# A mixer and feed-forward layer on one core: a conditioning row loaded later, conditioning steps loaded one ahead, and six reloads moved beside the last attention head

## The chip, the cores and the metric

The kernel runs on one core of a Trainium2 chip. The metric is the device time of one execution in microseconds (us); three runs of the kernel before gave a median of 1257.21 us (1256.59 to 1258.64).

## The reference, cut to what matters

One layer of a diffusion backbone over 512 latent tokens of width 1024, with a context of 256 tokens, all in float32. The conditioning vector `c` gives six modulation vectors; two are needed at once, the other four (first gate, second shift, second scale, second gate) only from the output projection on.

```python
mod = (silu_c @ w_ada[l] + b_ada[l])[:, None, :]
sh1, sc1, g1, sh2, sc2, g2 = jnp.split(mod, 6, axis=-1)
...
hm = head_norm(h_f + h_b, lp["m_norm_g"]) * o      # two-way mLSTM, four heads
hh = hyena(hv, (hx1, hx2), spec, lp["hy_skip"])    # long convolution, two orders
y = gm * (hm @ lp["w_pm"]) + gh * (hh @ lp["w_ph"])
return y @ lp["w_out"]
...
x = x + g1 * y
h2 = rmsnorm(x, norm2_g[l]) * (1.0 + sc2) + sh2
x = x + g2 * swiglu(h2, ffn_w1[l], ffn_w3[l], ffn_w2[l])
return rmsnorm(x, final_g)
```

## The kernel before, in words

Activations are held with features on the 128 partitions and the 512 tokens along the free axis, so a matrix of width 1024 is eight tiles of 128 x 512. Every product of two float32 matrices is made of three matmuls on operands split into a high and a low part (`mm3`, L214 to L217): ACT copies the high part, DVE subtracts it for the low part (`split`, L210 to L212). A tile of a projection (`gemm`) is 8 k-steps of three matmuls, 24 matmuls of 512 columns.

Weights come through `wsplit` (L221): a raw tile `wr` of 512 KB is loaded from SP's queue (L236), then split into `wh` and `wl`. Each of the three tags has four buffers. The `wr` buffers are also the staging slots of all other things that are split or used once: the heads' q, k and v (L886), and the conditioning steps. So at most four such loads are in flight or waiting to be used, whoever wants them.

The order on each engine is set by a scheduler in the program's build: it takes instructions by priority, which is the order in which the program makes them, with the loads and splits of weights 600 places ahead. In the trace the loads into `wr` leave SP in the program's order. Each queue then runs strictly in the order that was fixed. `issue_after` (`behind`) holds a group of instructions behind a given matmul of the same engine.

The stages that matter here, in order:

- **The Hyena convolution** in four channel blocks, in pool `ph`. Its last act is the store of two tiles `cx` into DRAM (hhd, L1237, from POOL's queue). Then the pool is closed (L1238) and its memory is given to the tile `crow` (pool `pc`) and to the heads' pool `pm`. The pool `pm` waits tile by tile for what lay there before (`reuse_waits="tile"`); `pc` waits for the whole of `ph`.
- **The conditioning row.** `ada_row` (L352) loads `c` broadcast to all partitions into `crow` (L354), takes a tanh on ACT into a `wr` slot (L355) and makes silu with two DVE instructions (L356, L357). It stands right behind the closing of the pool (L1240).
- **The conditioning steps.** `ada_later` (L339) is a generator: each `next` loads 512 KB of `w_ada` into a `wr` slot (L344), multiplies it by `crow` on DVE and adds it up along the free axis (L346, with a read of the accumulator). `background()` does one step; 24 steps are spread over the tiles of w_ph (8), w_pm (8) and w_out (5, then 3 at once), and 8 more over the first tiles of the feed-forward layer.
- **Left-over gate tiles.** Of the 28 tiles of q and gates that serve as fillers, six are left at the end of the Hyena stage; they are put between the loads, the decays and the scores of head 0 (`fill(next(cf))`, counts 2, 1, 0, 1, 1, 1). `sel` and `mask` are small tables that the decay rows need (L1280 to L1285); the decay rows are the matmuls L854.
- **The heads** (loop over `h`, L1315). `start(h + 1)` loads and splits the next head's q, k, v and makes its decays; `weigh` makes its scores; `values(h, 0)` and `values(h, 1)` are the two directions; `head_norm` normalises on DVE and POOL; `head_out` (made one head later by `late`) transposes on TensorE (L957), multiplies with the output gate read from DRAM (od, L962) and stores two tiles of hmd (L964, POOL's queue). Between them run the eight w_ph tiles (`ph_tiles`), three of them, with head 3's `head_out`, behind the loop.
- **w_pm** (L1351 on). `reload` reads the eight tiles of hmd back and splits them into buffers `big`; then for each of eight tiles a `gemm`, the gate (gmd) and the Hyena branch (y2d) on DVE (L1361, L1362), and a split into y.
- **w_out** and the norm behind it, then the feed-forward layer.

The lines of the old loop around the reload, and of the step:

```python
    hm = reload(hmd, big, big)
    for d in range(KT):
        wh, wl = wsplit(I["wpm"][d], [128, KT, 128])
        ps = bank(psG)
        gemm(ps, wh, wl, hm[0], hm[1], SEQ)
```

The tags that the change uses anew are `K` (two buffers of 128 x 2048, the split k of a head), `uh` and `ul` (two buffers of 128 x 1024 each, the split q of a head) and `s2` (six buffers of 128 x 512, everything short-lived).

Of the kernel before, what the change touches and what calls it, by code (L numbers as in the profile page):

```python
# [9 lines left out]
F32R = mybir.dt.float32r  # L10
# [6 lines left out]
SEQ = 512  # L17
CTX = 256
ROW = 64
NH = 4  # L20
DH = 256
DFF = 2816
KT = D // 128
# [133 lines left out]
def build(nc, tc, I, out, dbg=None):  # L157
# [4 lines left out]
    def pool(name, bufs=1, space=None, **kw):  # L162
        if space is not None:
            kw["space"] = space
        return tc.tile_pool(name=name, bufs=bufs, **kw)
# [16 lines left out]
    def T(p, shape, dt=F32, tag=None, bufs=None):  # L182
        uid[0] += 1
        p = HOME.get(tag, p)
        bufs = BUFS.get(tag, bufs)
        kw = {} if bufs is None else {"bufs": bufs}
        nm = f"{tag or 't'}_{uid[0]}"
        return p.tile(list(shape), dt, tag=tag or nm, name=nm, **kw)
# [9 lines left out]
    def bank(p=None):  # L198
        return T(p or psH, [128, 512], F32, "bank")
# [10 lines left out]
    def split(hi, lo, x):  # L210
        act.activation(hi, x, AF.Copy)  # L211
        dve.tensor_sub(lo, x, hi.bitcast(F32))  # L212
# [8 lines left out]
    def wsplit(src, shape):  # L221
        n = int(np.prod(shape[1:]))
        raw = T(PW, [128, WMAX], F32, "wr")
        hi = T(PW, [128, WMAX], F32R, "wh", 4)
        lo = T(PW, [128, WMAX], F32R, "wl", 4)

        def view(t):
            v = t[:, :n]
            return v if len(shape) == 2 else v.rearrange("p (a b) -> p a b", a=shape[1])

        with tc.high_priority(PR[0]):
            if isinstance(src, list):
                for s, sl in src:
                    dma(view(raw)[:, :, sl], s)
            else:
                dma(view(raw), src)  # L236
            split(hi[:, :n], lo[:, :n], raw[:, :n])
        return view(hi), view(lo)
# [6 lines left out]
    for key, shp in VECS:  # L245
        m = int(np.prod(shp))
        v = vecs[:, at : at + m]
# [91 lines left out]
    def ada_later(first, last):  # L339


        for j in range(first, last):
            w = T(PW, [128, WMAX], F32, "wr")[:, :D]
            dma(w, I["wada"][j])  # L344
            s = modT[:, 2 + j // KT, j % KT, 0:1]
            dve.scalar_tensor_tensor(w, w, 1.0, crow[:], op0=ALU.mult, op1=ALU.mult, accum_out=s)  # L346
            if j % KT == KT - 1:
                m = modT[:, 2 + j // KT, :, 0]
                dve.tensor_tensor(m, m, bada[:, 16 + j - KT + 1 : 16 + j + 1, 0], op=ALU.add)
            yield  # L350

    def ada_row():  # L352
        th = T(PW, [128, WMAX], F32, "wr")[:, :D]
        dma(crow[:], I["crow"].broadcast_to([128, D]))  # L354
        act.activation(th, crow[:], AF.Tanh, scale=0.5)  # L355
        dve.tensor_scalar_mul(crow[:], crow[:], 0.5)  # L356
        dve.scalar_tensor_tensor(crow[:], th, 1.0, crow[:], op0=ALU.add, op1=ALU.mult)  # L357
# [189 lines left out]
    def gemm(ps, wh, wl, xh, xl, n, ks=range(KT)):  # L547
        for k in ks:
            m = mm3(ps[:, :n], wh[:, k], wl[:, k], xh[k][:, :n], xl[k][:, :n], k == 0, k == KT - 1)
        tails.append(m.ins)  # L550

    def behind(lag=0):

        return tc.issue_after(tails[-1 - lag])
# [45 lines left out]
    hmd = T(PD, [128, KT, SEQ], F32, "hmd")  # L600
# [237 lines left out]
    def parts(dt=F32):  # L838
        return T(PM_, [128, 10, 128], dt, "dy"), T(PM_, [128, 8, 128], dt, "dx")
# [78 lines left out]
    def halves(Dm):  # L918
        wh, wl = parts(F32R), parts(F32R)
        for i in (1, 0):  # L920
            split(wh[i][:], wl[i][:], Dm[i][:])
        return wh, wl

    def values(h, d, W, V, den, hs):
        (wh, wl), (Vh, Vl) = W, V
        for t in range(4):
            ps = bank(psG)
            src = [4, 5] + [s for s in range(4) if (s <= t if d == 0 else s >= t)]
            for j, s in enumerate(src):
                b = t - PIECE[d][s][0]  # L930
                m = mm3(ps[:, :NV], piece(wh, d, s)[:, b], piece(wl, d, s)[:, b], Vh[:, s], Vl[:, s], j == 0, j == len(src) - 1)
            tails.append(m.ins)
            dn = den[:, d, t : t + 1]
            act.activation(dn, ps[:, 256:257], AF.Abs)
            dve.tensor_tensor(dn, dn, G["em"][:, d, t, h : h + 1], op=ALU.max)
            dve.reciprocal(dn, dn)
            if d == 0:
                act.activation(hs[:, t], ps[:, :256], AF.Copy, scale=dn)
            else:
                dve.scalar_tensor_tensor(hs[:, t], ps[:, :256], dn, hs[:, t], op0=ALU.mult, op1=ALU.add)  # L940
# [27 lines left out]
    PT = st.enter_context(pool("pt"))  # L968
# [155 lines left out]
    def fetch(o, c):  # L1124
        K = T(PH, [128, 2, 4, 256], F32, "K")
        dma(K[:], Kd[:, o, c])
        return K

    later = ada_later(0, 3 * KT)

    def background():
        next(later, None)
# [39 lines left out]
    def fill(n):  # L1172
        for _ in range(n):
            if fills:
                fills.pop(0)()

    def signal(c):
        u = (T(PH, [128, 4, 256], F32R, "uh"), T(PH, [128, 4, 256], F32R, "ul"))
        g1 = T(PH, [128, 4, 256], F32, "gx1", 1)

        def finish(which, i, cv):
            sl = slice(128 * i, 128 * i + 128)
            with behind():
                tk = to_tokens(cv)
            if which == 0:
                split(u[0][:, :, sl], u[1][:, :, sl], tk)
            else:
                act.activation(g1[:, :, sl], tk, AF.Copy)

        last = None  # L1190
        for which in range(2):
            for i in range(2):
                cv = hy_tile(PH, hT, which, 2 * c + i, "s2")
                if last:
                    finish(*last)
                last = which, i, cv
        return (u, g1), lambda: finish(*last)

    nxt, end = signal(0)
    fill(B0)  # L1200
    end()
    for c in range(4):
# [14 lines left out]
        v = (T(PH, [128, 4, 256], F32R, "uh"), T(PH, [128, 4, 256], F32R, "ul"))  # L1217
# [9 lines left out]
        if c < 3:  # L1227
            nxt, end = ahead[0]
# [8 lines left out]
                store(hhd[:, 2 * c + i], x2[i][:])  # L1237
    P1.close()  # L1238
    crow = T(st.enter_context(pool("pc")), [128, D], F32, "crow")
    ada_row()  # L1240
    cf = iter(CF)


# [2 lines left out]
    place(PM_, ("rrow", [128, 512]), ("mask", [128, 256]), ("identr", [128, 128]), ("sel", [128, 8]), ("selr", [128, 8]),  # L1246
          ("dy", [128, 1280]), ("dx", [128, 1024]))

    def reload(src, hi, lo):
        xs = ([], [])  # L1250
        for k in range(KT):
            t = scr()
            dma(t[:], src[:, k])
            xs[0].append(hi())
            xs[1].append(lo())
            split(xs[0][-1][:], xs[1][-1][:], t[:])
        return xs

    def scr():
        return T(PT, [128, SEQ], F32, "s2")  # L1260

    def slots(tag, dt=F32R):
        return lambda: T(PT, [128, SEQ], dt, tag)

    def ph_tiles():
        hh = reload(hhd, slots("hTh"), slots("hTl"))
        for d in range(KT):
            wh, wl = wsplit(I["wph"][d], [128, KT, 128])
            ps = bank(psG)
            gemm(ps, wh, wl, hh[0], hh[1], SEQ)  # L1270
            g = scr()
            dma(g[:], gmd[:, 1, d])
            dve.scalar_tensor_tensor(g[:], g[:], 1.0, ps[:], op0=ALU.add, op1=ALU.mult)
            store(y2d[:, d], g[:])
            background()
            yield
# [13 lines left out]
    def start(h):  # L1290
        L = heads.get(h) or load_head(h)
        return L, [decay(h, d) for d in range(2)]
# [2 lines left out]
    fill(next(cf))  # L1295
    weigh(0, L[0], L[1], Dm)
    fill(next(cf))
    W = [halves(Dm[d]) for d in range(2)]
    fill(next(cf))
    while fills:  # L1300
        fill(1)
    ph = ph_tiles()
    PHN = ((1, 0), (1, 1), (1, 1), (0, 0))
    done = []

    def beside(h, i):
        for _ in range(PHN[h][i]):
            next(ph)

    def late(_=None):  # L1310
        if done:
            with behind():
                head_out(*done.pop())

    for h in range(NH):  # L1315
        nxt = start(h + 1) if h + 1 < NH else None
        den = T(PM_, [128, 2, 4], F32, "den", 2)
        hs = T(PM_, [128, 4, 256], F32, "hs", 2)
        values(h, 0, W[0], L[2], den, hs)
        late(hs)  # L1320
        beside(h, 0)
        if nxt:
            weigh(h + 1, nxt[0][0], nxt[0][1], nxt[1])
        values(h, 1, W[1], L[2], den, hs)
        if nxt:
            Wn = [halves(nxt[1][d]) for d in range(2)]
        beside(h, 1)
        head_norm(hs)
        done.append((h, hs))
        if nxt:  # L1330
            L, W = nxt[0], Wn
    next(ph)
# [15 lines left out]
    def half(t, hf):  # L1348
        return t[:, 256 * hf : 256 * hf + 256]

    hm = reload(hmd, big, big)  # L1351
    y = ([], [])
    for d in range(KT):
        wh, wl = wsplit(I["wpm"][d], [128, KT, 128])
# [149 lines left out]
```

## Time and profile before

| | us |
|---|---|
| median of three runs | 1257.21 |
| the profiled execution, its own time | 1251.44 |
| its span, first to last instruction | 1249.6 |
| TensorE busy | 1197.4 (96%) |
| DVE busy | 835.6 (67%) |
| ACT busy | 529.5 (42%) |
| mean granted TensorE clock | 0.983 |

The profile is one execution. Busy times leave out instructions that only issue a load or wait on a semaphore. Idle time is put down to what released the engine last ("<-DVE hs L951": the wait ended when DVE's instruction of line 951 on tile hs was done). A matmul's listed duration overlaps the next one's; what one costs is the distance from start to start. PEclk is the share of TensorE's full clock of 2.4 GHz that was granted, averaged over a stretch.

### The profile page before, as it was taken

Reading aid. Unit: us, or ns where it says so; the run is one execution under the profiler, and the core shown is the slowest. Engines: PE = TensorE matmul, PEld = TensorE weight load, DVE = VectorE, ACT = ScalarE, POOL = GpSimd, SP = SyncE. Lnnn points to the kernel's source line nnn. Section 1 sums busy time; section 2 is a strip of 40 time slices with the busy share of each in tenths; the row PEclk is TensorE's granted clock in tenths of the full one; section 3 lists DMA queues with packets and bytes.
Section 4 is the critical chain, followed back from the end, with each engine's and each line's share of the span. In section 5 each row is a group of like instructions: output and inputs, shape, how many; then the busy total and the mean of one; then the engine's idle time right before and its main releaser. Section 6 shows DMA issues by size and latency. Waiting matters only on the chain. (4 is left out here: it accounts for less than half of the span.)

```text
span 1249.6 us, 16789 instructions
## 1 busy us (share of the span) xinstructions
PE 1197.4 (96%) x6440; PEld 1017.8 (81%) x6440; DVE 835.6 (67%) x1336; ACT 529.5 (42%) x824; POOL 68.2 (5%) x135
## 2 busy tenths in 40 slices
PE   4999999999999999997999998989999999999997
PEld 2799988888888888885788786868988888888886
DVE  6967798978989898874568795765754433432332
ACT  3754556654445454435466533322422322222231
POOL 0011110100000000000001111000000000000000
PEclk9999999999999999997999998999999999999998
DMA  9644442554342443206445657874443233223312
GB/s 356 226 169 149 157 168 94 183 188 135 117 153 79 158 135 135 77 34 220 146 153 175 222 196 238 301 233 135 143 154 100 93 101 101 89 88 97 102 47 68
DMA packets 61585, 184.83 MB, mean 148 GB/s; under 512 B 8504, under 2 KB 12352, under 8 KB 59328
## 3 DMA queue, kind: packets, MB, share of 16 engines
q1 hardware_dynamic: 53840, 154.38, 37.8%
q0 software_dynamic: 7664, 29.37, 6.4%
q8 instruction: 51, 0.84, 0.3%
q14 instruction: 30, 0.25, 0.1%
HBM read 152.26 MB, written 31.46 MB: 147 GB/s over the span
## 5 line engine op out<-in xcount | busy, mean ns | idle before, releaser
L215 PE MATMUL bank<-hTh,wh 128*128 128x512 f32 (+1 forms) x952 | 369.0, 389 | 2.9 <-ACT hTh L1057 1.9
L216 PE MATMUL bank<-hTl,wh 128*128 128x512 f32 (+1 forms) x952 | 368.0, 387 | 2.0 <-DVE hTl L1063 2.0
L217 PE MATMUL bank<-hTh,wl 128*128 128x512 f32 (+1 forms) x952 | 367.6, 387 | 0.0
L211 ACT ACTIVATE wh<-wr 128x1024 fp32r<-128x1024 f32 (+1 forms) x167 | 172.3, 1033 | 418.8 <-PE bank L216 215.1
L212 DVE TENSOR_TENSOR wl<-wr,wh 128x1024 fp32r<-128x1024 f32 (+1 forms) x167 | 198.1, 1188 | 175.9 <-ACT wh L211 174.3
L215 PEld LDWEIGHTS bank<-hTh,wh 128*128 128x128 f32 x952 | 179.9, 189 | 38.9 <-ACT hTh L1057 2.1
L216 PEld LDWEIGHTS bank<-hTl,wh 128*128 128x128 f32 x952 | 180.3, 189 | 36.7 <-DVE hTl L1063 2.5
L217 PEld LDWEIGHTS bank<-hTh,wl 128*128 128x128 f32 x952 | 180.0, 189 | 35.9 <-issue 0.4
L215 PE MATMUL bank<-big,wh 128*128 128x512 f32 (+1 forms) x314 | 115.7, 370 | 8.1 <-ACT big L211 8.1
L216 PE MATMUL bank<-big,wh 128*128 128x512 f32 (+1 forms) x314 | 116.3, 370 | 0.0
L217 PE MATMUL bank<-big,wl 128*128 128x512 f32 (+1 forms) x314 | 115.3, 367 | 0.0
L215 PEld LDWEIGHTS bank<-big,wh 128*128 128x128 f32 x314 | 60.6, 194 | 18.9 <-ACT big L211 9.9
L216 PEld LDWEIGHTS bank<-big,wh 128*128 128x128 f32 x314 | 61.1, 195 | 10.8 <-DVE big L212 1.6
L217 PEld LDWEIGHTS bank<-big,wl 128*128 128x128 f32 x314 | 61.0, 194 | 9.2
L346 DVE SCALAR_TENSOR_TENSOR wr<-wr,crow 128x1024 f32<-128x1024 f32 x32 | 39.0, 1220 | 32.2 <-DMA wr<-in_wada 32.1
L211 ACT ACTIVATE hb<-hb 128x512 fp32r<-128x512 f32 (+1 forms) x49 | 36.8, 768 | 29.3 <-DVE hb L442 17.7
L1448 DVE TENSOR_TENSOR s<-s,bank 128x512 f32<-128x512 f32 x22 | 15.1, 686 | 46.7 <-PE bank L217 46.7
L212 DVE TENSOR_TENSOR hb<-hb,hb 128x512 fp32r<-128x512 f32 (+1 forms) x49 | 40.3, 860 | 2.0 <-ACT hb L211 2.0
L211 ACT ACTIVATE big<-s 128x512 fp32r<-128x512 f32 x34 | 21.1, 623 | 43.0 <-DVE s L1362 29.6
L635 PE MATMUL bank<-wh,hTl 128*128 128x256 f32 (+1 forms) x128 | 36.4, 284 | 0.0
L633 PE MATMUL bank<-wh,hTh 128*128 128x256 f32 (+1 forms) x128 | 36.4, 284 | 0.0
L634 PE MATMUL bank<-wl,hTh 128*128 128x256 f32 (+1 forms) x128 | 36.4, 284 | 0.0
(367 smaller groups left out, 2086.2 us busy)
## 6 DMA issues: line engine op xcount, KB each, us to landing
wr<-in_win SPq DMA_DIRECT2D x64, 512.0 KB, 3.8
wr<-in_w SPq DMA_DIRECT2D x60, 512.0 KB, 3.6
wr<-in_wada SPq DMA_DIRECT2D x32, 512.0 KB, 4.4
Kd<-K POOLq DMA_DIRECT2D x8, 1024.0 KB, 4.8
K<-Kd SPq DMA_DIRECT2D x8, 1024.0 KB, 5.8
wr<-in_wv SPq DMA_DIRECT2D x8, 512.0 KB
gmd<-s POOLq DMA_DIRECT2D x16, 256.0 KB, 2.5
wr<-in_wph SPq DMA_DIRECT2D x8, 512.0 KB, 3.6
```

The lines of the kernel that those rows point to most:

```text
L211: act.activation(hi, x, AF.Copy)
L212: dve.tensor_sub(lo, x, hi.bitcast(F32))
L215: pe.matmul(o, wh, xh, start=first, stop=False)
L216: pe.matmul(o, wh, xl, start=False, stop=False)
L217: return pe.matmul(o, wl, xh, start=False, stop=last)
L346: dve.scalar_tensor_tensor(w, w, 1.0, crow[:], op0=ALU.mult, op1=ALU.mult, accum_out=s)
L633: pe.matmul(o, xh, wh, start=bool(k == 0), stop=False)
L634: pe.matmul(o, xh, wl, start=False, stop=False)
L635: m = pe.matmul(o, xl, wh, start=False, stop=bool(k == KT - 1))
L1448: dve.tensor_tensor(t[:], t[:], pb[:], op=ALU.mult)
```

## The change

Three things are done. `ada_row` is called behind the scores of head 0 instead of right behind the closing of the Hyena pool. `ada_later` loads the first step's weights at its first `next` (for which one more `background()` is called before the heads), and each step then loads the next one's before it uses its own. And in head 3, behind head 2's `head_out`, tiles 0 to 5 of hmd are reloaded into the buffers of `K`, `uh` and `ul`, which no head needs any more; tiles 6 and 7 are reloaded where all eight were.

```diff
     def ada_later(first, last):
-        for j in range(first, last):
+        def wada(j):
             w = T(PW, [128, WMAX], F32, "wr")[:, :D]
             dma(w, I["wada"][j])
+            return w
+
+        nxt = wada(first)
+        yield
+        for j in range(first, last):
+            w = nxt
+            if j + 1 < last:
+                nxt = wada(j + 1)
             s = modT[:, 2 + j // KT, j % KT, 0:1]
             dve.scalar_tensor_tensor(w, w, 1.0, crow[:], op0=ALU.mult, op1=ALU.mult, accum_out=s)
...
     crow = T(st.enter_context(pool("pc")), [128, D], F32, "crow")
-    ada_row()
     cf = iter(CF)
...
-    def reload(src, hi, lo):
+    def reload(src, hi, lo, ks=range(KT)):
         xs = ([], [])
-        for k in range(KT):
+        for k in ks:
...
     weigh(0, L[0], L[1], Dm)
     fill(next(cf))
+    ada_row()
     W = [halves(Dm[d]) for d in range(2)]
     fill(next(cf))
     while fills:
         fill(1)
     ph = ph_tiles()
+    background()
...
         late(hs)
+        if h == NH - 1:
+            sp_ = [T(PT, [128, 2048], F32R, "K") for _ in range(2)]
+            parts_ = [[v[:, 512 * j : 512 * j + 512] for j in range(4)] for v in sp_]
+            for i, tag in enumerate(("uh", "ul")):
+                v = T(PT, [128, 2, SEQ], F32R, tag)
+                parts_[i] += [v[:, 0], v[:, 1]]
+            its = [iter(v) for v in parts_]
+            hm = reload(hmd, lambda: next(its[0]), lambda: next(its[1]), range(6))
         beside(h, 0)
...
-    hm = reload(hmd, big, big)
+    rest = reload(hmd, big, big, range(6, KT))
+    hm = hm[0] + rest[0], hm[1] + rest[1]
```

## Rows read from the trace of the kernel before

**Rows 1.** The page, part 1: busy time of each engine.
```profile
PE 1197.4 (96%) x6440; PEld 1017.8 (81%) x6440; DVE 835.6 (67%) x1336; ACT 529.5 (42%) x824; POOL 68.2 (5%) x135
```
**Rows 2.** Table by stretch: length, PE, PEld, DVE, ACT, POOL busy (instructions), PEclk, DMA, GB/s.
```profile
900.00:1100.00 200.00, 200.00 (x884) 165.68 (x883) 84.68 (x102) 56.97 (x73) 0.00 (x0) 1.00 0.35 110
566.97:587.93 20.96, 11.65 (x32) 7.84 (x32) 8.74 (x8) 11.18 (x18) 0.47 (x4) 0.67 0.75 255
766.79:780.92 14.13, 10.54 (x29) 6.96 (x30) 8.23 (x13) 6.16 (x10) 0.54 (x1) 0.76 0.88 306
818.90:831.49 12.59, 8.03 (x29) 6.10 (x28) 10.30 (x18) 2.59 (x4) 0.00 (x0) 0.87 0.68 228
600.00:620.00 20.00, 19.80 (x88) 16.07 (x87) 12.43 (x18) 10.77 (x21) 0.88 (x2) 1.00 0.21 73
740.00:755.40 15.40, 13.30 (x87) 11.84 (x86) 12.36 (x44) 3.67 (x10) 4.27 (x7) 1.00 0.63 222
```
**Rows 3.** Timeline of TensorE: start, duration, line, tiles, count [idle before <-releaser].
```profile
574.70 0.80 PE L854 MATMUL bank<-rrow,sel 16*128 16x512 f32 x4 [7.72 <-ACT sel L1282]
576.87 0.79 PE L854 MATMUL bank<-rrow,sel 16*128 16x512 f32 x1 [1.38 <-ACT dx L860]
...
755.46 0.44 PE L957 MATMUL bank<-mats,hs 128*128 128x128 f32 x2 [0.76 <-DVE hs L951]
770.05 0.69 PE L215 MATMUL bank<-big,wh 128*128 128x512 f32 x1 [3.26 <-ACT big L211]
828.13 1.18 PE L215 MATMUL bank<-big,wh 128*128 128x512 f32 x2 [4.56 <-ACT big L211]
```
**Rows 4.** Waits in SP's queue, 510 to 580 us: total, times, longest.
```profile
SPq L354 <- DMA hhd<-cx: 54.8, 1, 54.8
```
**Rows 5.** Timeline of SP's queue: two neighbouring issues.
```profile
514.43 0.33 SPq L236 DMA_DIRECT2D wr<-in_win  x1
569.70 0.33 SPq L354 DMA_DIRECT2D crow<-in_crow  x1
```
**Rows 6.** Timeline of ACT: the tanh of the conditioning row.
```profile
573.49 1.06 ACT L355 ACTIVATE wr<-crow 128x1024 f32<-128x1024 f32 x1 [5.37 <-DMA crow<-in_crow]
```
**Rows 7.** Timeline of DVE: the two instructions of the conditioning row.
```profile
574.58 0.69 DVE L356 TENSOR_SCALAR crow<-crow 128x1024 f32<-128x1024 f32 x1 [8.24 <-ACT wr L355]
575.30 1.23 DVE L357 SCALAR_TENSOR_TENSOR crow<-wr,crow 128x1024 f32<-128x1024 f32 x1
```
**Rows 8.** DVE's groups by line, 781 to 829 us: busy, mean ns | idle before.
```profile
L346 DVE SCALAR_TENSOR_TENSOR wr<-wr,crow 128x1024 f32<-128x1024 f32 x10 | 12.2, 1224 | 9.8 <-DMA wr<-in_wada 9.8
...
L212 DVE TENSOR_TENSOR big<-s,big 128x512 fp32r<-128x512 f32 x8 | 5.5, 688 | 2.1 <-ACT big L211 2.1
```
**Rows 9.** Waits in SP's queue, 764 to 832 us: total, times, longest.
```profile
SPq L236 <- DVE wr L346: 14.5, 9, 3.7
...
SPq L344 <- DVE wr L346: 6.7, 2, 3.4
```
**Rows 10.** Timeline of POOL: two stores of hmd, of tiles 5 and 7.
```profile
747.66 0.54 POOL L964 DMA_DIRECT2D hmd<-s  x1 [0.85 <-DVE den L936]
764.33 0.54 POOL L964 DMA_DIRECT2D hmd<-s  x1 [1.03 <-DVE s L963]
```
**Rows 11.** DMA issues of the whole span: size, median us from issue to landing.
```profile
wr<-in_wout SPq DMA_DIRECT2D x8, 512.0 KB, 5.2
...
hmd<-s POOLq DMA_DIRECT2D x8, 256.0 KB, 4.5
s<-hmd SPq DMA_DIRECT2D x8, 256.0 KB, 3.8
```
**Rows 12.** The page, part 5: the splits of weights and of activations.
```profile
L211 ACT ACTIVATE wh<-wr 128x1024 fp32r<-128x1024 f32 (+1 forms) x167 | 172.3, 1033 | 418.8 <-PE bank L216 215.1
L212 DVE TENSOR_TENSOR wl<-wr,wh 128x1024 fp32r<-128x1024 f32 (+1 forms) x167 | 198.1, 1188 | 175.9 <-ACT wh L211 174.3
...
L211 ACT ACTIVATE big<-s 128x512 fp32r<-128x512 f32 x34 | 21.1, 623 | 43.0 <-DVE s L1362 29.6
```

## The prediction

> **What bounds the kernel now.** The page's busy times come first [rows 1]: TensorE is busy 1197.4 of 1249.6 us, no other engine above 67%. So two things can be won: time in which TensorE stands still, 52.2 us in all, and time in which it runs below full clock. Next the table by stretch [rows 2]: from 900 to 1100 us nothing is lost, and 884 matmuls in 200.00 us give 0.226 us for one at full clock. By this price three stretches, cut from the last matmul before a stop to the end of the tile behind it, lose 20.96 - 32 x 0.226 = **13.7**, 14.13 - 29 x 0.226 = **7.6** and 12.59 - 29 x 0.226 = **6.0 us**: 27.3 us. TensorE's own timeline [rows 3] splits them: stops of 7.72 + 1.38, of 3.26 and of 4.56 us, and the rest, 10.4 us, is half clock: their granted clock is 0.67, 0.76 and 0.87 of 2.4 GHz on average, so parts ran at 1.2 GHz, while 900 to 1100 us shows 1.00. No other stop behind 560 us reaches 2 us, and what is lost before 560 us the diff does not touch.
>
> **Part one: the row of the conditioning steps moves behind the scores of head 0.** Why TensorE stops at 567 us is in SP's queue [rows 4, 5]: one issue, the row crow at L354, waits 54.8 us for the store hhd<-cx, because its memory is the Hyena pool's and that pool is free only when its last store has landed. SP takes its issues in order, so nothing leaves it from 514.43 to 569.70 us, and the six gate tiles that were kept to fill TensorE here have no weights. ACT is blocked in the same way [rows 6]: its tanh on the row waits 5.37 us for the load, and the copy of sel right behind it is what TensorE's 7.72 us waits for. After the change selr, the gate tiles' weights and head 0's loads stand behind nothing of the kind; they wait only for staging slots, which the splits free one by one. Taken out: 13.7 us. Not all comes back: the 1.38 us wait for ACT's exponentials, and I keep 0.8 us of it. **Term: -12.9.** Bounds: 8.3 (only the stops, 9.1 - 0.8; the half clock entered all the same) to 13.7.
>
> What is moved is one 512 KB load on SP, one tanh on ACT (1.06 us), two DVE instructions (0.69 + 1.23 us) [rows 6, 7] and the tanh's staging slot. At the new place they lie beside head 0's scores and splits: there DVE is busy 12.43 and ACT 10.77 of 20 us, TensorE 19.80 [rows 2]. That slack hides them; without it they would cost their 3.0 us. The Hyena pool has been free since 569.70 by then, so the long wait has nothing left to wait for.
>
> **Part two: steps loaded one ahead.** The steps' DVE instruction L346 waited for its load 9.8 us over ten instructions between 781 and 829 us [rows 8], and DVE's lag is what TensorE waits for at 828.13: the first w_out tile needs the last y tile. But the loads are not held back by their place in the program. In SP's own waits [rows 9] the weights' L236 waited 14.5 us for L346 and the steps' L344 6.7 us for L346: each leaves when one of four staging slots comes free. Loading one ahead leaves that turn-taking as it is and shifts it by one place: one step fewer stands in the crowded stretch. I count one instruction with its mean wait, 1.22 + 0.98 = **2.2 us off the stop at 828 us**, and leave the half clock behind it. Bounds: 0 (the turn-taking absorbs it) to 6.0 (all waits gone). A loss by it is the last rival. The eight steps behind 832 us only have their DVE instruction moved by one tile, beside a TensorE that stops for none of them: 0.
>
> **Part three: six of eight hm tiles are reloaded beside head 3.** Now all eight loads stand behind head 3's last store, and from 766.79 us TensorE has nothing else. With six tiles at hand w_pm's first tile starts at once: 18 matmuls x 0.226 = 4.1 us, to 770.9. Tile 7 can't come earlier: its store is issued at 764.33 [rows 10] and lands in a median 4.5 us, its load in 3.8 [rows 11], then an ACT split of 0.62 [rows 12]: ready at 773.3, and three matmuls are wanted for tile 6 ahead of it. So between 0 (a second w_pm tile fills in) and 1.9 us of stop remain; I take 1.3, and no half clock for it, since the stretch from 740 us, with TensorE idle for 2.1 us in pieces, kept clock 1.00 [rows 2].
>
> The Trainium skill would have this rest at nil: DMA: Bandwidth & Descriptors, section Anatomy of one DMA — SWDGE (gpsimd) path, puts a transfer at about 2.0 us plus its bytes by 436 GB/s; my estimate from it is 2.6 us for 256 KB, each way, and tile 7 would be there at 770.2. By that the sum would be 1.3 us better; the rows say 4.5 and 3.8, and they decide.
>
> What it adds beside head 3: six loads on SP, of which the last two wait for head 2's stores with the loads for head 3's output, gates, steps and w_pm weights queued behind; six splits on ACT (0.62 us each) and six on DVE (0.69 each [rows 8], 4.1 us). From 740 to 755.4 us DVE is busy 12.36 of 15.40 us [rows 2], and its head normalisation is what TensorE waits for at 755.46 [rows 3]. 3.0 us are idle, so 1.1 us spill over. Upper bound: the DVE split of tile 5 stands in front of the normalisation. That tile's store is issued at 747.66 [rows 10]; plus 4.5 + 3.8 + 0.62 + 0.69 it is split at 757.3. At worst DVE stands from the issue to there, 9.6 us, of which 3.0 were idle anyway: 6.6 us late, with 1.5 us of half clock as behind the stop at 828. Lower bound 0. I take 1.1, as DVE's idle time is the nearest row. **Term: -7.6 + 1.3 + 1.1 = -5.2.** Bounds: -7.6 to -7.6 + 1.9 + 6.6 + 1.5 = +2.4.
>
> **Sum.** -12.9 - 2.2 - 5.2 = **-20.3 us**. The profiled execution took 1251.44 us (1249.6 of span and 1.8 around it) and would become 1231.1. The median of the runs, 1257.21, stands 5.8 above it; I carry that over: **1236.9 us**. A measurement of this kernel can tell about 0.2% (2.5 us) from no change.
>
> **Rivals.**
> *Everything pays* (27.3 us): no rest, no delay at head 3, no stop at 828 us. For it: 1.5 MB of loads leave the stretch from 764 us. Against: the slots bind. 1229.9; chance 0.10.
> *Head 3 takes it back*: SP stands behind the store of tile 5 and DVE behind its split, part three ends at +2.4, and the lag on DVE eats part two: 1257.2 - 12.9 + 2.4 = 1246.7. For it: both queues go in order, as L354 and the tanh show. Against: the idle 3.0 us. 0.20.
> *The stops go, the half clock stays*: 8.3 + (3.26 - 2.4 = 0.9) + 2.2 = 11.4 us, 1245.8. Against: no half clock without a stop in the three stretches. 0.04. The Trainium skill leans this way (TensorE: Matmul & The Clock Gate, section What's actually happening): it puts the ramp's penalty under 1% of a span, varying by run, and advises against fitting it. The trace agrees on the size (10.4 us are 0.8%); I count them.
> *Part one does not do what it says*: the tanh's staging slot still comes ahead of the last weights, SP and TensorE stop again at the new place, and parts two and three alone pay 7.4: 1249.8, or no difference if they fail too. 0.08.
> *Slower: the slots starve the weights.* A step's tile that waits a whole step holds one of four slots; if others are late in the same way, each weight pays its whole cycle in series: load 5.2 us (w_out's median [rows 11]), ACT 1.03, DVE 1.19 [rows 12], 7.4 us against 24 x 0.226 = 5.4 us of TensorE, 2.0 lost on each tile. It decides from the twelfth of the 16 tiles of w_pm and w_out on (24 us against 20.3 + 2.5); with all 16 the time is 1236.9 + 32 = 1269. For it: L236 already waits 14.5 us for L346. Against: four wh and four wl buffers stand between a load and its matmuls. 0.08.
> My forecast keeps 0.50.
>
> **How the numbers follow.** 1229 to 1249 us holds the forecast, the first three rivals, and part one's lower end with nothing else won (8.3 us: 1248.9): 0.84. Faster: 0.50 + 0.10 + 0.20 + 0.04 + half of 0.08 = 0.88; same: the other half, 0.04; slower: 0.08.
>
> **What would show it.** Part one is right if L354 no longer waits some 50 us for hhd, weights leave SP between 520 and 569 us, and TensorE runs through 567 to 588 us at clock 1.00. Part three is right if w_pm starts within 1 us of the last w_ph tile and pauses only before tiles 6 or 7; wrong if head 3's transposes wait several us for DVE. Part two is right if L344 and L236 still wait for L346, and the stop before the last y tile is shorter but there. I am wrong in the main if 560 to 590 us still holds the long stop, or if ACT's wh waits for DMA all through w_pm.

## The result, and the profile after

The changed kernel takes **1246.26 us** (median of six runs, 1244.43 to 1248.38); the kernel before, on the same chip, 1256.76 (six runs, 1251.47 to 1258.64). The ratio is 0.9925 [0.9901, 0.9948], a gain of 9.4 us against the 20.3 of the forecast. The time lies inside the range and 9.4 us above the forecast, next to the rival "Head 3 takes it back" (1246.7).

The two profiled executions differ by less, 1251.44 against 1246.66 us; most of the reason is told at the end. The table by stretch, first one row of the kernel before, then four of the changed kernel (columns as in [rows 2]), and the changed kernel's TensorE timeline (as in [rows 3]):

```profile
560.00:640.00 80.00, 70.49 (x318) 54.98 (x317) 37.11 (x52) 46.41 (x87) 5.03 (x12) 0.91 0.55 184
```

```profile
560.00:640.00 80.00, 79.99 (x398) 64.25 (x397) 45.91 (x72) 47.39 (x89) 5.59 (x13) 1.00 0.48 153
645.00:657.00 12.00, 11.43 (x45) 8.99 (x44) 8.24 (x24) 7.75 (x22) 3.06 (x4) 0.57 0.49 165
744.50:763.20 18.70, 14.78 (x59) 11.58 (x57) 13.04 (x27) 5.81 (x9) 4.99 (x7) 0.82 0.73 240
763.20:781.00 17.80, 12.31 (x42) 9.58 (x41) 7.43 (x10) 3.89 (x5) 1.08 (x2) 0.81 0.85 282
```

```profile
744.58 0.38 PE L965 MATMUL bank<-mats,hs 128*128 128x128 f32 x2
745.84 0.44 PE L965 MATMUL bank<-mats,hs 128*128 128x128 f32 x2 [0.88 <-DVE hs L959]
750.25 0.69 PE L965 MATMUL bank<-mats,hs 128*128 128x128 f32 x2 [3.04 <-DVE hs L959]
756.75 0.38 PE L965 MATMUL bank<-mats,hs 128*128 128x128 f32 x2
...
773.07 0.80 PE L215 MATMUL bank<-big,wh 128*128 128x512 f32 x1 [5.49 <-ACT big L211]
...
822.38 0.73 PE L215 MATMUL bank<-big,wh 128*128 128x512 f32 x2 [2.22 <-ACT big L211]
```

Lines behind L347 have moved by eight: L957 is L965 now, L951 is L959, L346 is L354. What to see: from 560 to 640 us TensorE loses nothing (79.99 of 80.00; the same window of before held 70.49 at clock 0.91). Then a stretch at half clock that the first profile did not have. Then head 3's transposes, four pairs that stood side by side before ([rows 3] has the last at 755.46), come one by one between w_ph's matmuls, with two waits for the normalisation. And w_pm starts at once at 763.11, does 19 matmuls (18 on tiles 0 to 5 and one of its next tile) and stops for 5.49 us, longer than the 3.26 us that it replaces.

How far the changed kernel is ahead at the same piece of work, in the two profiled executions:

| at | before | after | ahead |
|---|---|---|---|
| values of head 0 start | 626.01 | 613.25 | 12.8 |
| first of head 3's transposes | 753.78 | 744.58 | 9.2 |
| last w_ph matmul ends | 766.79 | 763.27 | 3.5 |
| TensorE resumes before the last y tile | 828.13 | 822.38 | 5.8 |
| span | 1249.6 | 1244.9 | 4.7 |

Part one delivers; 12.8 to 9.2 is the half clock; 9.2 to 3.5 is lost around head 3, in the part that was to gain 5.2.

### The profile page after: what moved, and what is told of

Same layout as the page of the kernel before. It is cut to its first block, busy times and chain, and to the rows that moved or that the text cites. A ratio compares the mean times of both kernels' runs of the same rounds, so it can differ in the third digit from the quotient of the medians.

```text
span 1244.9 us, 16797 instructions
## 1 busy us (share of the span) xinstructions
PE 1198.9 (96%) x6440; PEld 1020.4 (82%) x6440; DVE 835.5 (67%) x1336; ACT 529.4 (43%) x824; POOL 69.2 (6%) x135
## 4 chain that ended last, share of the span: by engine, by line
PE 86%; DMA 5%; DVE 4%; issue 2%; ACT 1%; POOL 1%; SPq 0%; DVEq 0%; POOLq 0%; ACTq 0%
PE bank L215 25%; PE bank L216 25%; PE bank L217 25%; DMA wr<-in_wada 3%; PE bank L641 2%; PE bank L642 2%; PE bank L643 2%; DMA s<-hmd 1%; PE bank L862 1%; DVE wl L212 1%; PE bank L445 1%; PE bank L598 1%; PE bank L446 1%; DMA wr<-in_wph 0%; DMA ul<-in_xT 0%
## 5 line engine op out<-in xcount | busy, mean ns | idle before, releaser
L215 PE MATMUL bank<-big,wh 128*128 128x512 f32 (+1 forms) x266 | 96.1, 362 | 7.7 <-ACT big L211 7.7
L216 PE MATMUL bank<-big,wh 128*128 128x512 f32 (+1 forms) x266 | 96.6, 363 | 0.3 <-DVE big L212 0.3
L217 PE MATMUL bank<-big,wl 128*128 128x512 f32 (+1 forms) x266 | 96.0, 361 | 0.0
L215 PEld LDWEIGHTS bank<-big,wh 128*128 128x128 f32 x266 | 51.2, 193 | 15.8 <-ACT big L211 8.6
L216 PEld LDWEIGHTS bank<-big,wh 128*128 128x128 f32 x266 | 51.5, 194 | 8.0 <-DVE big L212 0.7
L217 PEld LDWEIGHTS bank<-big,wl 128*128 128x128 f32 x266 | 51.5, 194 | 7.3
L354 DVE SCALAR_TENSOR_TENSOR wr<-wr,crow 128x1024 f32<-128x1024 f32 x32 | 39.0, 1220 | 22.9 <-DMA wr<-in_wada 22.9
L373 POOL TENSOR_TENSOR rr<-rv,negh 128x2 f32<-128x2 f32 (+1 forms) x6 | 4.5, 756 | 526.4 <-DVE rv L371 526.4
```

Source lines behind the costliest of these rows:

```text
L215: pe.matmul(o, wh, xh, start=first, stop=False)
L216: pe.matmul(o, wh, xl, start=False, stop=False)
L217: return pe.matmul(o, wl, xh, start=False, stop=last)
```

## The experiments

The theories that the expectations name: **T**, that parts one and two pay as forecast, and the reload costs because its splits stand ahead of head 3's normalisation on DVE and spread the transposes. **T1 and T2** split T (SP's wait for head 2's stores, or the order on DVE whatever SP does). **U**, that part two takes back what part one wins. **L**, that the half clock near 650 us belongs to the single execution; its rival **V**, that it is a price of the earlier row. In e13 and e14, T2 and **T3** stand for something else, two theories of what the last y tile waits for; their expectations say it. In all, with ratios to the kernel before on the same chip:

| kernel | parts | median us | ratio [95%] | resumes before last y, after a stop of |
|---|---|---|---|---|
| e1_row | one | 1242.7 | 0.9893 [0.9863, 0.9922] | 820.57, 4.13 |
| e11_steps | two | 1251.35 | 0.9975 [0.9958, 0.9992] | 824.05, 3.68 (no row) |
| e12_reload | three | 1256.75 | 1.0015 [0.9991, 1.0039] | 829.22, 3.15 (no row) |
| e2_row_steps | one, two | 1239.77 | 0.9876 [0.9853, 0.99] | 817.37, 1.86 |
| e10, the same | one, two | 1241.2 | 0.9884 [0.9857, 0.991] | 817.19, 5.39 |
| e3_row_reload | one, three | 1244.52 | 0.9906 [0.988, 0.9932] | 817.61, 3.33 (*) |
| e7, the change | all | 1246.12 | 0.9942 [0.9922, 0.9963] | 821.56, 2.51 |
| e4_late | all, reload late | 1241.49 | 0.9883 [0.9857, 0.9909] | 813.20, 3.38 (*) |
| e6_row_late | one, reload late | 1241.04 | 0.9888 [0.9866, 0.9911] | 817.75, 2.50 |
| e5_four | all, four tiles early | 1242.56 | 0.9911 [0.989, 0.9931] | 818.95, 1.51 |
| e9_four_late | all, four tiles late | 1242.32 | 0.9899 [0.9874, 0.9925] | 816.95, 6.03 |
| e13 | e9, steps in w_out | 1238.67 | 0.987 [0.9846, 0.9895] | 809.40, 1.26 |
| e14 | e10, steps in w_out | 1240.19 | 0.9877 [0.9848, 0.9905] | 811.54, 1.63 |

(*) a profile without the half clock near 650 us, some 4 us early from there on; so are e11 and e12, which lack the row's 13 us.

**Part one; one and two; one and three.** e1 undoes the other two parts, e2 the reload, e3 the steps. The core of e1, against the kernel before:

```diff
-    ada_row()
     cf = iter(CF)
...
     weigh(0, L[0], L[1], Dm)
     fill(next(cf))
+    ada_row()
```

> Part one alone (the conditioning row moved), the rest as before. Theory T (part one pays in full, the early reload at head 3 takes part of it back): 12.8 us faster than before, some 1244 us on the median, faster than the whole change by about 3; TensorE runs through 560 to 640 us without a stop, and from head 3 on the trace looks as before, shifted by 12 to 13 us, or by some 8 where the half clock is entered near 646 us. Rival U (it is the steps loaded one ahead that take it back): also 1244. Rival V (the half clock that the changed kernel shows from 646 to 656 us comes from part one's shift): 8 to 9 us faster, 1248, with the half clock there in the profile as well.

> Parts one and two, no early reload. T: part two is worth 0 to 2 us, so 1242 to 1244 us, and head 3's transposes stop TensorE for under 1.5 us as before. U: the steps cost some 3 us, 1247, with loads of weights or of head 3's gate later than in the run with part one alone. V: as the run with part one alone, less at most 2.

> Parts one and three, the steps not loaded ahead. T: as slow as the whole change or a little slower, 1246 to 1248 us; head 3's last transposes wait for DVE several us later than w_ph's first tile there, and w_pm stops for some 5 us before its tile 6. U: 1241 or less, as part three pays its 5 us. V: 1248 for the clock, with or without part three.

Part one alone is worth 1256.13 x 0.0107 = 13.4 us. With part two the ratio falls by 0.0017 (2.1 us); with the reload instead it rises by 0.0013 (1.6 us). These steps are smaller than the intervals; the single parts below are measured against before itself. T's order of the three holds, but its times for e2 and e3 are some 2 us too high, and its wait at head 3's transposes is too short for e2 (1.97 us, not under 1.5). U falls, as e2 is not slower than e1. V falls as a price that is always paid: the profiles of e1 and e2 have the half clock (0.83 and 0.77 from 640 to 670 us), that of e3 has 1.00, and all three have the row. Whether the row makes it more frequent stays open: ten of the twelve profiles with the row have it, and one of the four without (e8, below).

**The reload behind the normalisation.** e4 is the whole change with the block of the reload moved by a few lines; the same loads and splits remain:

```diff
         late(hs)
-        if h == NH - 1:
-            ...
-            hm = reload(hmd, lambda: next(its[0]), lambda: next(its[1]), range(6))
         beside(h, 0)
...
         head_norm(hs)
         done.append((h, hs))
+        if h == NH - 1:
+            ...
+            hm = reload(hmd, lambda: next(its[0]), lambda: next(its[1]), range(6))
```

> The whole change, but the six reloads stand behind head 3's normalisation in the program instead of ahead of its second direction, so that the normalisation's instructions on DVE and the loads of head 3's gate go first. T: no stop of over 1.5 us at head 3's transposes, the stop before w_pm's tile 6 under 3 us instead of 5.5, and 5 to 8 us faster than the whole change: 1238 to 1241. U: no faster than the whole change, 1245 to 1247. V: as U plus what the clock does.

The median falls from 1246.26 to 1241.49 us, the ratio from 0.9925 (0.9942 the second time) to 0.9883. The place, and nothing else, cost 5 to 7 us (e4's interval is clear of that of the second measurement and just overlaps that of the first). One number of T missed: the last transposes still wait 2.28 us for the normalisation, not under 1.5. In e2 and e10, which reload nothing early, they wait 1.97 us, in e1 0.64: some 2 us of this wait come with part two (in e2 a step stands on DVE ahead of the last normalisation), and by themselves they do not make the kernel slow. e6 is the late reload without part two:

> The row moved and the six tiles reloaded behind head 3's normalisation, steps not loaded ahead: the fourth corner to the kernels measured with the row alone (1242.7), the row and steps ahead (1239.8), and the whole change with the late reload (1241.5). If the parts add, 1241.5 + 2.9 = 1244.4 us. If steps loaded ahead and a late reload work on the same stops (the late w_pm tiles), the late reload pays here alone: 1241 to 1242 us, and loading ahead then pays nothing on top.

1241.04 us: the late reload pays here what part two pays in e2, and the two together (e4) pay no more than one. e6 also settles what in the order hurts. The changed kernel first, in three timelines: DVE, with the splits of the reload (K, ul) and the normalisation (L959); SP, with the loads of the reload and those of head 3's output gates; POOL, with the stores of head 3's output:

```profile
747.30 1.29 DVE L212 TENSOR_TENSOR K<-s,K 128x512 fp32r<-128x512 f32 x2
749.17 0.69 DVE L212 TENSOR_TENSOR ul<-s,uh 128x512 fp32r<-128x512 f32 x1 [0.59 <-ACT uh L211]
749.78 0.41 DVE L959 TENSOR_SCALAR hs<-hs,mv,rs 128x256 f32<-128x256 f32 x1
750.12 1.23 DVE L212 TENSOR_TENSOR wl<-wr,wh 128x1024 fp32r<-128x1024 f32 x1
751.28 0.69 DVE L212 TENSOR_TENSOR ul<-s,uh 128x512 fp32r<-128x512 f32 x1
...
754.91 0.41 DVE L959 TENSOR_SCALAR hs<-hs,mv,rs 128x256 f32<-128x256 f32 x1 [0.45 <-POOL rs L958]
```

```profile
738.70 8.87 SPq L1260 DMA_DIRECT2D s<-hmd  x4
...
754.87 0.90 SPq L970 DMA_DIRECT2D s<-od  x2
```

```profile
762.00 1.15 POOL L972 DMA_DIRECT2D hmd<-s  x2 [7.12 <-DVE s L971]
```

Timelines of e6: SP's issue of the same four loads, TensorE's last transposes, POOL's last store.

```profile
737.30 8.89 SPq L1252 DMA_DIRECT2D s<-hmd  x4
```

```profile
745.19 0.82 PE L957 MATMUL bank<-mats,hs 128*128 128x128 f32 x6
746.43 0.44 PE L957 MATMUL bank<-mats,hs 128*128 128x128 f32 x2 [0.42 <-DVE hs L951]
```

```profile
758.00 0.54 POOL L964 DMA_DIRECT2D hmd<-s  x1 [2.11 <-DVE s L963]
```

And DVE's product with the gate ahead of that store:

```profile
757.02 0.69 DVE L963 SCALAR_TENSOR_TENSOR s<-s,s 128x512 f32<-128x512 f32 x1 [0.83 <-DMA s<-od]
```

SP stands just as long in e6 (8.89 against 8.87 us, for head 2's stores). But the transposes stay together and end ten microseconds earlier, and the last store leaves at 758.00 instead of 762 to 763 us. So it is not SP's stand that spreads the transposes. It is not without effect: e6's last store waits for a gate that SP loads behind the stand, and leaves at 758.00, where e1, the same without a reload, issues both stores from 756.16; but e6's time, 1241.04 us against 1242.7, shows no loss by it. In the changed kernel all six splits have gone ahead of DVE's last normalisation (754.91), in e6 three (its last is at 745.97); and w_ph's matmuls are put between the transposes that wait for it. The splits are not alone there: a weight's split and a step (1.23 us each) stand among them, and the last normalisation also waits for an instruction of POOL, behind a store of y2d. Which share of the delay each of these has was not measured.

**Four tiles instead of six.** e5 reloads only the tiles whose stores landed long before, at the early place; e9 does so at the late place:

```diff
-            hm = reload(hmd, lambda: next(its[0]), lambda: next(its[1]), range(6))
+            hm = reload(hmd, lambda: next(its[0]), lambda: next(its[1]), range(4))
...
-    rest = reload(hmd, big, big, range(6, KT))
+    rest = reload(hmd, lambda: next(its[0], None) or big(), lambda: next(its[1], None) or big(), range(4, KT))
```

> The whole change, but only tiles 0 to 3 reloaded beside head 3 (heads 0 and 1, whose stores landed long before); 4 to 7 behind it. T1 (what hurts is the wait for head 2's stores: loads of tiles 4 and 5 stand in SP's queue and their splits block DVE ahead of the normalisation): no split waits for a store any more, head 3's transposes stop TensorE by less than 1 us in all, time 1239 to 1241 us. T2 (any split put ahead of the normalisation delays it, and tiles late for w_pm are the bound): four splits of 0.7 us instead of six, so about two thirds of the loss of 6.5 us stays: 1243 to 1245 us.

T1 falls on its own number: no split of DVE waits for a store any more, and TensorE still waits 2.85 us for the normalisation, behind a step and two K splits. T2 holds for that wait; the time (1242.56) lies between the bands of the two: half of the loss comes back, since the last store leaves 3.3 us earlier (758.72) and w_pm's stop breaks up into seven waits of 3.0 us in all.

> Parts one and two, and tiles 0 to 3 alone reloaded, behind head 3's normalisation; 4 to 7 with the rest. T (the order on DVE is what hurt; loads of tiles 4 and 5 that wait for head 2's stores hold SP for some 7 us at little cost): no load of SP waits over 3 us for a store between 735 and 750 us, the transposes stand together, 1239 to 1241 us, within 2 us of the late reload of six (1241.5). T1 (SP's wait for head 2's stores costs by itself, since the loads of head 3's output gates stand behind it): 1236 to 1238.5 us, below parts one and two alone.

1242.32 us, T's side, a little above its band; T1 falls again. SP's longest wait for a store is 4.9 us, not below 3: a gate tile waits for the `s2` buffer that such a store empties. The find is in TensorE's stretches and in its next stop (table by stretch, then timeline):

```profile
763.00:805.00 42.00, 42.00 (x187) 34.76 (x186) 29.12 (x43) 11.38 (x15) 0.54 (x1) 1.00 0.83 290
```

```profile
816.95 1.22 PE L215 MATMUL bank<-big,wh 128*128 128x512 f32 x2 [6.03 <-ACT big L211]
```

w_pm now runs without any stop at clock 1.00, just what part three was to bring, and TensorE then waits 6.03 us for the last y tile, which comes at 817 us as in e2, e6 and e10. In e1, with neither part two nor a reload, it comes at 820.57; so part two or a late reload brings this date forward by some 3 us, and both together by no more. From there on it is not set by when w_pm starts.

**Controls.** e10 is e2 on another chip, expected at 1238.5 to 1241 us with head 3's last store near 754 us; it took 1241.2, and the two stores leave from 752.21. The two profiles of this one program stop 1.86 and 5.39 us ahead of the last y tile, and resume at 817.37 and 817.19: the length of that stop is no measure, the date is. The change and the kernel before once more:

> The changed kernel once more, as the control on this chip. T (the reload beside head 3 delays head 3's normalisation and w_pm stops for the last tiles) and every rival expect the time measured before, 1244 to 1248 us. The profile should again hold waits of TensorE for the normalisation on DVE of over 2 us between 740 and 760 us, and a stop of 4 to 6 us inside w_pm. L (half clock near 646 to 656 us is a matter of the single execution) allows the half clock to be there or not; if it hangs on the change, it is there.

> The kernel before, profiled a second time. L (the half clock behind the short stops near 650 us is a matter of the single execution): a run near the median of 1257 us shows a stretch at half clock that the first profile (1251.4 us) did not have, somewhere the two traces hold the same work, of some 4 to 6 us of lost time. Rival: no such stretch, and the difference of 5 us between runs is spread over many transfers.

e7 gives 1246.12 us, with waits of 0.95 and 2.52 us for the normalisation, a stop of 5.23 us in w_pm and the half clock. e8 (one run, 1254.68 us) shows that the kernel before has it too, in another execution. The same 12 us of work, first the first profile, then e8:

```profile
656.50:668.50 12.00, 10.93 (x72) 8.94 (x73) 9.95 (x31) 9.69 (x29) 3.05 (x4) 1.00 0.44 143
```

```profile
656.50:668.50 12.00, 10.93 (x42) 7.75 (x42) 10.52 (x27) 9.61 (x24) 3.26 (x7) 0.69 0.33 108
```

TensorE is busy 10.93 us in both, with 72 matmuls in one and 42 in the other. L holds, though the time lost (3.3 us, worked out at the end) is below its 4 to 6. It is not the chip either: e2, e4 and e7 have parts one and two, all on one chip, and show a granted clock of 0.77, 1.00 and 0.83 from 640 to 670 us.

**Part two alone, part three alone**, each on the kernel before:

> Part two alone on the kernel before: the row stays where it was and nothing is reloaded early. T (loading ahead only shifts the turns on the staging slots by one place): 1 to 3 us below the kernel before of the same chip, ratio 0.998. Rival (with the row late, TensorE's stop at 567 us hides what part two wins): no difference, ratio 0.999 to 1.001.

> Part three alone on the kernel before. T (the splits stand ahead of head 3's normalisation on DVE; the transposes are spread, the last store of head 3 comes some 7 us late, and w_pm stops for the last two tiles instead of for the first): the stop of 3.3 us at w_pm's start goes and one of 4 to 6 us some 18 matmuls later comes; 0 to 3 us above the kernel before, ratio 1.000 to 1.002. Rival (the forecast's term, -5.2 us): ratio 0.996, and the cost seen in the whole change came from part two and part three together.

Part two is worth 1254.95 x 0.0025 = 3.1 us [1.0, 5.3]: T's number (the rival's near end, 0.999, is still inside the interval). Where the time is won is another matter. The table by stretch around w_pm's start and around the last y tile, first of the kernel before, then of e11:

```profile
755.00:790.00 35.00, 30.95 (x119) 23.57 (x120) 20.14 (x29) 11.03 (x15) 2.74 (x5) 0.90 0.82 276
818.00:835.00 17.00, 12.44 (x48) 9.71 (x47) 13.38 (x21) 3.90 (x5) 0.00 (x0) 0.90 0.71 227
```

```profile
755.00:790.00 35.00, 31.73 (x130) 25.29 (x131) 21.50 (x30) 11.58 (x16) 2.97 (x6) 0.95 0.88 302
818.00:835.00 17.00, 13.32 (x51) 10.34 (x50) 10.57 (x17) 4.01 (x5) 0.00 (x0) 0.90 0.72 238
```

TensorE does 11 more matmuls around w_pm's start (11 x 0.226 = 2.5 us) and 3 more around the last y tile (0.7 us). The loads of hmd leave SP from 760.76 instead of 764.00 us, and the stop of 3.26 us at w_pm's start has become three of 0.85, 0.22 and 1.47 us. Part three is worth nothing: +1.9 us [-1.1, +4.9], and the forecast's 0.996 lies outside its interval. Its TensorE timeline:

```profile
758.50 0.44 PE L957 MATMUL bank<-mats,hs 128*128 128x128 f32 x2 [2.20 <-DVE hs L951]
763.20 0.44 PE L957 MATMUL bank<-mats,hs 128*128 128x128 f32 x2 [0.39 <-DVE hs L951]
...
778.96 0.79 PE L215 MATMUL bank<-big,wh 128*128 128x512 f32 x1 [4.63 <-ACT big L211]
```

The last transposes come at 763.20 instead of 755.46 [rows 3], with no other part of the change in place, and the stop at w_pm's start has become one of 4.63 us inside it.

**What holds the last y tile.** In e9 DVE waits for the steps' loads, so e13 takes the calls that stand beside w_pm and puts them beside w_out, two a tile; e14 does the same without any reload.

```diff
         split(y[0][-1][:], y[1][-1][:], g[:])
-        background()
...
             background()
-    for _ in range(LAST):
+            background()
+    for _ in range(2 * LAST):
         background()
```

> The late reload of four tiles, parts one and two, with the eight steps beside w_pm moved to w_out (two beside each tile instead of one). T2 (what TensorE waits for before the last y tile, at 817 us in every version, is DVE waiting for the steps' loads through w_pm): that stop, 6.0 us with the steps there, falls below 1.5 us and w_out's first tile goes on near 812 us; as w_out then carries two steps a tile, some of it comes back there, 1236 to 1240 us. T3 (the y tiles are held by w_pm's weights or by their own chain of load, split and add, whatever the steps do): TensorE still stops 4 us or more before the last y tile.

> Parts one and two, no early reload, with the eight steps beside w_pm moved to w_out in the same way. T2: the first w_pm tiles still stop 1.5 to 2.5 us in pieces for the late attention tiles, the stop before the last y tile (5.4 us) falls below 1.5 us; 1237 to 1241 us, 0 to 2 us above the one with four tiles reloaded late, since only without the steps does the early reload pay. T3: no change against the same kernel with its steps in w_pm (1241.2 us).

DVE's group of the steps, from w_pm's start to the last y tile, in e9 (763 to 817.5 us) and in e13 (763 to 811 us); then e13's resumption before the last y tile:

```profile
L354 DVE SCALAR_TENSOR_TENSOR wr<-wr,crow 128x1024 f32<-128x1024 f32 x11 | 13.5, 1224 | 11.2 <-DMA wr<-in_wada 11.2
```

```profile
L354 DVE SCALAR_TENSOR_TENSOR wr<-wr,crow 128x1024 f32<-128x1024 f32 x9 | 10.9, 1223 | 5.1 <-DMA wr<-in_wada 5.1
```

```profile
809.40 0.50 PE L215 MATMUL bank<-big,wh 128*128 128x512 f32 x1 [1.26 <-ACT big L211]
```

T2 holds in the date, though the edit did less than it says: the scheduler draws steps forward, and nine instead of eleven still lie in the stretch, which is 6.5 us shorter (up to 809 us both kernels have eight). What changed is that DVE waits less for them, 5.1 us instead of 11.2; the last y tile comes at 809.40 instead of 816.95 us, and the stop falls from 6.03 to 1.26 us. The steps share staging slots and DVE's order with w_pm's tiles, and that turn-taking dated the last y tile. Some comes back: from 830 to 880 us TensorE is busy 47.92 of 50 us in e9 and 44.23 in e13. In e14 the late attention tiles still cost 2.0 us in five waits, and the stop is 1.63 us, just above T2's 1.5. In time T2 is not shown: e14 is 1.0 us below e10 and e13 3.6 below e9, on different chips, and in both pairs the intervals of the ratios overlap. e13 (1238.67 us, 0.987) has the lowest median of all, 1.5 us below e14; it beats both kernels, but its interval overlaps that of e2, which has neither reload nor moved steps.

## Why the prediction was wrong

**Part one was right**: -12.9 forecast, 12.8 us in the two traces at head 0's values, 13.4 us as a ratio. TensorE ran through the stretch at clock 1.00, weights left SP between 520 and 569 us, and the tanh and DVE's two instructions (1.06, 0.69 and 1.23 us, as in [rows 6, 7]) were hidden. One sentence of it failed at no cost: the pool was not yet free. The load of the row left SP at 570.08, only 0.38 us later than before [rows 5], and still waited for hhd. This is SP's queue from 505 to 590 us in the changed kernel:

```profile
SPq L362 <- DMA hhd<-cx: 6.7, 1, 6.7
```

So 54.8 us [rows 4] became 6.7, not nothing; TensorE did not stop for the weights behind it.

**Part two had the right size alone, in good part by luck, and was lost in company.** -2.2 forecast, 3.1 measured. SP still waits for steps and weights in turn, as the working had it, and over the forecast's stretch, shifted by e11's lead of 4 us (777 to 825 us), nine steps stand instead of ten, with DVE's waits down from 9.8 to 7.1. But the stop at 828 us, from which the 2.2 us were to come, only shrinks from 4.56 to 3.68 us. Most of the gain, 2.5 us, is at w_pm's start, where the working looked for none. In the whole change part two gains nothing (e3 0.9906 without it, the change 0.9925 and 0.9942 with it). The traces suggest why: parts two and three take the same stop, and where part two has taken it (e2 stops there in pieces of 1.9 us in all, e1 of 5.9), an early reload has little left to win and its cost on DVE stays. That reading is argued, not isolated.

**Part three is the step that failed**: "-7.6 + 1.3 + 1.1 = -5.2". Alone it measures +1.9. Two of its terms are wrong.

*The 1.1 us of spill on DVE.* I weighed six splits against DVE's idle time, as if they filled gaps. They were placed by program order, ahead of the normalisation, and with the normalisation late the scheduler put 4 and 17 of w_ph's matmuls ahead of the last two pairs of transposes. The last pair came at 756.75 us, where 755.46 less the lead of 9.2 us gives 746.3: 10.5 us late, not 1.1. I had named this order as the upper bound, 6.6 us, and chose the idle time as "the nearest row"; the bound itself was too low, as it counted only the wait for tile 5 and left the order on TensorE out.

*The 1.3 us of rest.* (Its upper bound, 1.9, is 1.7 by its own rows: 773.3 - 770.9 - 3 x 0.226.) It took the stores of tiles 6 and 7 at their old places. The late transposes moved them: 764.33 [rows 10] less 9.2 is 755.1, and the two were issued from 762.00. The chain of the changed kernel from the first of them, by start and duration, then reads:

```profile
762.00 5.32 DMA hmd<-s
...
767.38 4.98 DMA s<-hmd
...
772.38 0.64 ACT big L211
```

So w_pm stopped for 5.49 us, and half clock followed: 42 matmuls in 17.80 us lose 17.80 - 42 x 0.226 = 8.3 us, against the 7.6 that were to go. The transfers were slower than my medians (4.5 and 3.8 us, [rows 11]) too. The Trainium skill (DMA: Bandwidth & Descriptors, Anatomy of one DMA — SWDGE (gpsimd) path), from which I had an estimate of 2.6 us each way, is further off in this stretch, where the 16 DMA engines were 0.82 busy (the row from 763.20 us).

**And one thing was not asked:** what is late next. I let the stop at 828 us shrink by part two and stay for part three. e9 shows that a w_pm without a stop finds the last y tile at the same 817 us and waits 6.03 us for it. Even well placed, part three gains nothing measurable on top of part two (e4 and e9 against e2); with the steps moved out of the way it gains 1.5 us (e13 against e14), still inside the intervals.

**The rivals.** "Head 3 takes it back" came out in its number (1246.7) and its main mechanism, DVE behind the splits ahead of the normalisation. But it had DVE stand and wait for tile 5, behind SP's wait for the store; in the trace DVE waited 0.59 us for the high part of a reloaded tile there and was busy for most of the rest, and e6 has SP's wait without the loss. "Slots starve the weights" did not happen. The half clock went with the stop at 567 us, against "The stops go, the half clock stays".

## What to carry to other kernels

Before moving work into an engine's idle time, ask where in that engine's order it lands: a few microseconds of splits ahead of a short instruction that others wait for cost more than their own length, and the same work a few lines later cost nothing measurable. A stop that is taken out only pays if the next thing awaited is not already dated by something else; look for the next stop of the same engine and for who sets its date. Two edits that each shorten the way to the same date do not add.

## What the runs showed of the hardware that was not expected

The same kernel enters half clock in one execution and not in another, behind the same two short stops. TensorE's timeline in the first profile of the kernel before, then in e8:

```profile
657.37 0.59 PE L215 MATMUL bank<-vh,dx 128*128 128x258 f32 x3 [0.50 <-issue]
658.54 0.50 PE L854 MATMUL bank<-rrow,sel 16*128 16x512 f32 x1 [0.57 <-ACT dx L860]
```

```profile
658.61 0.59 PE L215 MATMUL bank<-vh,dx 128*128 128x258 f32 x3 [0.50 <-issue]
659.78 0.50 PE L854 MATMUL bank<-rrow,sel 16*128 16x512 f32 x1 [0.57 <-ACT dx L860]
```

Stops of 0.50 and 0.57 us in both, and a granted clock of 1.00 against 0.69 behind them. e8 is 1.2 us behind at these rows and 4.5 us at the last of head 2's transposes (745.97 against 741.46 us): 3.3 us. That is over half of the distance between the first profile of before and the median of its runs, and the same stretch in the changed kernel (0.57 from 645 to 657 us) takes 12.8 - 9.2 = 3.6 us from the lead of the changed kernel: most of the reason why the two profiled executions differ by only 4.8 us. The Trainium skill (TensorE: Matmul & The Clock Gate, What's actually happening) says that the ramp to full clock varies by run and costs under 1% of a typical span. The trace agrees in both, here for a stretch in the middle of a program: it came in one execution and not in the other, and 3.3 us are 0.3%. But that is as large as the parts that were to be told apart. A sum that starts from a single profiled execution should be checked for such a stretch first.
